# One transformer layer on one core: the low parts of some weights made by ACT and an adding DMA, and two more tiles of FFN 2 as pair jobs

## The chip, the cores and the metric

The kernel runs on one core of one Trainium2 chip. The metric is the device time of one execution in microseconds (us). The time before is 1120.33 us, the median of three runs (1120.18 to 1120.45).

## The reference

One layer of a streaming encoder, batch 1, 512 positions, width 1024, all in float32:

```python
f = swiglu(rms_norm(h, ffn1_pre_g), ffn1_w1, ffn1_w3, ffn1_w2)   # (silu(x@w1) * (x@w3)) @ w2, inner width 2816
h = h + 0.5 * rms_norm(f, ffn1_post_g)
u = rms_norm(h, mix_pre_g)
q, k, v, xr, xg = split(u @ w_in)
y_a = (rg_lru(causal_conv(xr)) * gelu(xg)) @ w_lru_out
y_b = swa_sink_attention(q, k, v, sinks, bias) @ w_attn_out
g = sigmoid(u @ w_gate + b_gate)
merged = g[:, :, 0] * y_a + g[:, :, 1] * y_b
h = h + rms_norm(merged @ w_o, mix_post_g)
f = swiglu(rms_norm(h, ffn2_pre_g), ffn2_w1, ffn2_w3, ffn2_w2)
h = h + 0.5 * rms_norm(f, ffn2_post_g)
```

## The kernel before

**Products in three terms.** Every float32 matrix product is made of three products of reduced float32 (float32r). Each operand x is split into a high part, the rounded copy, and a low part, x minus the high part. The product is wh·xh + wl·xh + wh·xl. A weight tile comes by a raw load of 512 KB on the SP queue (`dma_one`, L142). ACT makes the high part with a copy (L160 in `split_to`, L195 in `split2`), and DVE makes the low part with a subtraction (L161, L196). `get(name, i, ahead)` keeps loads and splits ahead of the use.

**Units.** `unit` makes 128 of the output columns for all 512 positions: 8 slices of the inner dimension times 3 terms, which is 24 matmuls of 128x512 (`mm_feat`, L205 to L207).

**Pairs.** The class `Pairs` treats two tiles of 128 columns together by a Strassen-Winograd scheme. Each weight matrix of such a pair is one job with 7 products in place of 8, each of 12 matmuls of 128x256 (`mm_s`, L845 to L847). `prep(m, i)` makes the weights of job m in five steps: i = 0 the sums S12 and S34 (four DVE operations), 1 the parts of the raw tile itself (`ra`), 2 those of S12, 3 those of S34, 4 those of a quarter (w22). `run` makes a job's products one after the other and calls the steps of the next job in between. The input side (sums of x by `sums`, tiles t1 to t4) is made once.

**Stages.** FFN 1 has 22 tiles: 6 as units, and 16 in 16 pair jobs (`NC1` = 6). The mixing follows (recurrent branch, attention, gates), then w_attn_out ("wao", 8 units from 684.73 us on), w_o ("wo", from 728.25 us), and FFN 2: tiles 0 and 1 at the end of `tok_gemm` for w_o, tiles 2 and 3 as four units (`swiglu_units`, `NC2` = 4), then 18 pair jobs. The gemm with w2 closes each FFN. Some partial products of w2 are made early (`PRE_AT`) and kept in DRAM (pre_w2b).

**Order.** Instructions are issued in the order of the code. `later(n, fn, rank)` puts work off by n points, and `point()` marks them, two in each unit and one after each product of a job. Work tiles come from a pool of 43 slots (`NSLOT`) of 128x1024; a slot is free again when the last reader of its tile is done. GpSimd (POOL) makes few operations: the low part OL of the attention output (L1481), and the issue of some DMAs.

Of the kernel before, what the change touches and what calls it, by code (L numbers as in the profile page):

```python
# [15 lines left out]
P = 128  # L16
# [35 lines left out]
def hybrid_layer(ctx: ExitStack, tc: tile.TileContext, a: dict, out: bass.AP):  # L52
# [22 lines left out]
    def f32(ap):  # L75
        return ap.bitcast(F32)
# [73 lines left out]
    def split_to(n):  # L150
        while st["split"] < min(n, len(order)) and st["split"] not in paired:
            k = st["split"]
            if k in apart:
                st["split"] += 1
                continue
            dma_to(k + 1)
            r = raws.pop(k)
            hi = slot([P, D], F32R, name="whi")
            lo = slot([P, D], F32R, name="wlo")
            act.activation(hi, r, AF.Copy)  # L160
            dve.tensor_tensor(out=lo, in0=r, in1=f32(hi), op=ALU.subtract)  # L161
            pairs[k] = (hi, lo)
            st["split"] += 1

# [14 lines left out]
    def later(n, fn, rank=1):  # L179
        uid[0] += 1  # L180
        due.append((now[0] + n, rank, uid[0], fn))
# [11 lines left out]
    def split2(hi, lo, src):  # L193

        act.activation(hi, src, AF.Copy)  # L195
        dve.tensor_tensor(out=lo, in0=src, in1=f32(hi), op=ALU.subtract)  # L196

    def mm_feat(ps, w, c0=0, c1=SEQ, xh=None, xl=None, ks=range(KT)):

# [11 lines left out]
    def unit(nm, i, **kw):  # L211
        w = get(nm, i)
        ps = bank("f")
        mm_feat(ps, w, **kw)
        return ps
# [269 lines left out]
    def pre_at(where):  # L485
        for nm, f, at_, step in PRE_AT.get(where, ()):
            pre_pair(nm, f, at_, step)
# [298 lines left out]
    def silu_mul(ps1, ps3, R=None, hid=None):  # L786

        t = slot([P, 2, SEQ], name="sw")
        f = len(hid.f) if hid else None
        if f is not None and f in hid.apart:  # L790
            if f - f % 2 not in hid.c:
                hid.c[f - f % 2] = slot([P, 2, SEQ], name="cc")
            o = hid.c[f - f % 2][:, f % 2, :]
        else:
            o = t[:, 1, :]
        if R is None:
            act.activation(t[:, 0, :], ps1, AF.Silu)
            dve.tensor_tensor(out=o, in0=ps3, in1=t[:, 0, :], op=ALU.mult)
        else:
            dve.tensor_tensor(out=t[:, 0, :], in0=ps1, in1=R, op=ALU.mult)  # L800
            dve.tensor_tensor(out=t[:, 1, :], in0=ps3, in1=R, op=ALU.mult)
            act.activation(t[:, 0, :], t[:, 0, :], AF.Silu)
            dve.tensor_tensor(out=o, in0=t[:, 1, :], in1=t[:, 0, :], op=ALU.mult)
        return o
# [45 lines left out]
    class Pairs:  # L850
# [13 lines left out]
        def prep(self, m, i):  # L864
            if m >= len(self.jobs):
                return
            k = self.k0 + 2 * m
            if i == 0:
                if k not in loaded or k + 1 not in loaded:
                    self.raws(m)  # L870
                s12, s34 = slot([P, 2 * QH], name="S12"), slot([P, 2 * QH], name="S34")
                self.w[m] = {"r": (raws.pop(k), raws.pop(k + 1)), "s": (s12, s34)}
            W = self.w[m]
            (ra, rb), (s12, s34) = W["r"], W["s"]
            a11, a12, a21, a22 = ra[:, :QH], ra[:, QH:], rb[:, :QH], rb[:, QH:]

            def both(src, w=2 * QH):
                hi = slot([P, w], F32R, name="whi")
                lo = slot([P, w], F32R, name="wlo")
                split2(hi, lo, src)  # L880
                return hi, lo

            def halves(p, a, b):
                W[a] = p[0][:, :QH], p[1][:, :QH]
                W[b] = p[0][:, QH:], p[1][:, QH:]

            if i == 0:
                dve.tensor_tensor(out=s12[:, :QH], in0=a21, in1=a22, op=ALU.add)
                dve.tensor_tensor(out=s12[:, QH:], in0=s12[:, :QH], in1=a11, op=ALU.subtract)
                dve.tensor_tensor(out=s34[:, QH:], in0=a12, in1=s12[:, QH:], op=ALU.subtract)  # L890
                dve.tensor_tensor(out=s34[:, :QH], in0=a11, in1=a21, op=ALU.subtract)
            elif i == 1:
                halves(both(ra), "a11", "a12")
            elif i == 2:
                halves(both(s12), "s1", "s2")
            elif i == 3:
                halves(both(s34), "s3", "s4")
            elif i == 4:
                t = slot([P, 2, QH], F32R, name="w22")
                split2(t[:, 0, :], t[:, 1, :], a22)  # L900
                W["a22"] = t[:, 0, :], t[:, 1, :]
                del W["r"], W["s"]

        def run(self, tail, hooks={}):
# [4 lines left out]
            for n, (nm, f) in enumerate(self.jobs):  # L909
# [8 lines left out]
                at = lambda i: [f() for f in hooks.get((n, i), ())]  # L918
                mm_s(W["a11"], X["b11"], bu)
                act.activation(q1, bu, AF.Copy)  # L920
                if n == len(self.jobs) - 1:
                    tail()
                at(1)
                mm_s(W["s1"], X["t1"], bx)
                act.activation(q5, bx, AF.Copy)
                at(2)
                last()
                self.prep(n + 1, 1)
                mm_s(W["s2"], X["t2"], bu, True)
                del W["s1"], W["s2"]  # L930
                act.activation(u, bu, AF.Copy)
# [53 lines left out]
    def load_x(k, q=sp):  # L985
        q.dma_start(out=xts[k // 2][:, k % 2, :], in_=a["xT"][k * P : (k + 1) * P, :])

    def load_w(u, kp):
        nm, i = order[u]
        c = slice(kp * 2 * P, (kp + 1) * 2 * P)  # L990
        sp.dma_start(out=raw3[u][:, c], in_=a[nm][i * P : (i + 1) * P, c])


    warm = slot([P, 512], F32R, name="warm")
# [3 lines left out]
        pe.matmul(psw, warm[:, :P], warm, start=True, stop=True)  # L998

    load_x(0, act)  # L1000
    sp.dma_start(out=vec, in_=a["vec"])
    for kp in range(KT // 2):
        load_w(0, kp)
        if kp:
            load_x(2 * kp)
        load_w(1, kp)
        load_w(2, kp)
        load_x(2 * kp + 1)
    dma_to(NS + 2)
# [54 lines left out]
    pairs_a.prep(0, 0)  # L1064
    ps.append(unit("w3a", 1))
    pairs_a.prep(0, 1)
    p1 = unit("w1a", 2)
    pairs_a.prep(0, 2)

# [54 lines left out]
    def swiglu_units(na, nb, f0, f1, hid, R=None, p1=None):  # L1124
        for f in range(f0, f1):
            p1, p3 = p1 or unit(na, f), unit(nb, f)
            later(1, lambda p1=p1, p3=p3: hid.f.append(silu_mul(p1, p3, R, hid)))
            p1 = None

    def uview(hh, th):  # L1130

        return lambda e, k: uT[:, e, 4 * hh + k, th * 256 : th * 256 + 256]
# [1 line left out]
    def pair_view(p):  # L1134
        return lambda e, k: p[e][:, k, :]

    def sums(xf):

        t = [slot([P, 4, 256], name="T") for _ in range(4)]
        dve.tensor_tensor(out=t[0], in0=xf[0, 1], in1=xf[0, 0], op=ALU.subtract)  # L1140
        dve.tensor_tensor(out=t[2], in0=xf[1, 1], in1=xf[0, 1], op=ALU.subtract)
        dve.tensor_tensor(out=t[1], in0=xf[1, 1], in1=t[0], op=ALU.subtract)
        dve.tensor_tensor(out=t[3], in0=xf[1, 0], in1=t[1], op=ALU.subtract)
        return t

    def to_slots(src):
        p = slot([P, 4, 256], F32R, name="Xh"), slot([P, 4, 256], F32R, name="Xl")
        split2(p[0], p[1], src)
        return pair_view(p)
# [363 lines left out]
    w = get("wao", 0)  # L1513
    point(True)
    pre_at("wao")
    xh = [OH[k // 2][:, k % 2, :] for k in range(KT)]
    xl = [OL[k // 2][:, k % 2, :] for k in range(KT)]
    mg = []
# [18 lines left out]
    bs = tok_gemm("wo", mg, KT, RO, "mix_post_g", 1.0, "ffn2_pre_g", [("w1b", 0), ("w3b", 0), ("w1b", 1), ("w3b", 1)], h1, h2, xf=xf)  # L1537


    hid = Hidden("w2b")  # L1540
    X2, tn = {"b11": uview(0, 0), "b21": uview(1, 0), "b22": uview(1, 1)}, []
    later(1, lambda: hid.f.append(silu_mul(bs[0], bs[1])))
    later(2, lambda: hid.f.append(silu_mul(bs[2], bs[3])))
    later(1, lambda: tn.extend(sums(xf)))
    later(2, lambda: xf.clear())
    for i in range(3):
        later(2 + i, lambda i=i: X2.update({f"t{i + 1}": to_slots(tn[i])}))
    pairs_b = Pairs("w1b", "w3b", NC2, X2, hid)
    end = 2 * 2 * (NC2 - 2)
    for i, at_ in enumerate((end - 7, end - 4, end - 3, end - 2, end - 1)):  # L1550
        later(at_, lambda i=i: pairs_b.prep(0, i))
    later(end, lambda: pairs_b.prep(1, 0))
    swiglu_units("w1b", "w3b", 2, NC2, hid)
    point(True)
    X2["t4"] = to_uT(tn[3], 0, 1)
    tn.clear()
    pairs_b.run(w2_ahead)
    X2 = pairs_b = None
    w2_gemm("w2b", hid, "ffn2_post_g", 0.5, None, [], h2, None)


# [9 lines left out]
SCAN_LAG = (1, 2, 3, 4, 6, 7, 9, 10)  # L1571
NSLOT = 43
RO = 6
W2 = {"w2a": (6, (4,), 6, 0.95), "w2b": (2, (4, 4), 4, 0.95)}
TR_K = {"w2a": 2, "wo": 4}
PRE = {"w2b": (2, 4, 6, 8, 14)}
PRE_AT = {"xr": [("w2b", 2, 2, 2), ("w2b", 8, 8, 2)], "xg": [("w2b", 4, 7, 1)], ("wg", 13): [("w2b", 6, 1, 1)], "wao": [("w2b", 14, 4, 1)]}
W2_LOAD = (14, 9, 8, 8)
P0A, P0B = 6, 8
W2_LEAD = 2.5  # L1580
W2_RAW = 4
W2_FLUSH = 2.5

NC1 = 6
NC2 = 4


# [52 lines left out]
```

## Time and profile before

| | us |
|---|---|
| median of three runs | 1120.33 |
| the profiled execution | 1120.09 |
| its span | 1118.3 |
| PE busy | 1109.7 (99%) |
| DVE busy | 907.3 (81%) |
| ACT busy | 607.8 (54%) |
| POOL busy | 34.7 (3%) |

The granted TensorE clock was 0.999 of full speed. A row of a group names the line, the engine, the operation, output<-input, the shapes and the count, then busy time, mean ns of one and the idle time before it. A row of waits gives who waited for what: us in total, times, the longest. A row of the timeline begins with the start and the duration in us. A row of windows begins with the stretch and its length, then has the busy time of PE, PEld (weight loads), DVE, ACT and POOL with their instruction counts, the granted clock, the share of the DMA engines' time and GB/s. A row of DMA issues ends with the KB of one and the median us from issue to landing.

### The profile page before, as it was taken

Reading aid. Unit: us, or ns where it says so; the run is one execution under the profiler, and the core shown is the slowest. Engines: PE = TensorE matmul, PEld = TensorE weight load, DVE = VectorE, ACT = ScalarE, POOL = GpSimd, SP = SyncE. Lnnn points to the kernel's source line nnn. Section 1 sums busy time; section 2 is a strip of 40 time slices with the busy share of each in tenths; the row PEclk is TensorE's granted clock in tenths of the full one; section 3 lists DMA queues with packets and bytes.
Section 4 is the critical chain, followed back from the end, with each engine's and each line's share of the span. In section 5 each row is a group of like instructions: output and inputs, shape, how many; then the busy total and the mean of one; then the engine's idle time right before and its main releaser. Section 6 shows DMA issues by size and latency. Waiting matters only on the chain.

```text
span 1118.3 us, 17215 instructions
## 1 busy us (share of the span) xinstructions
PE 1109.7 (99%) x6613; PEld 987.7 (88%) x6613; DVE 907.3 (81%) x1609; ACT 607.8 (54%) x1072; POOL 34.7 (3%) x60
## 2 busy tenths in 40 slices
PE   9999999999999999999999999999999999999997
PEld 7889999988889887888888888888999999998886
DVE  5999888888887777886799877777868888887995
ACT  7555555564455368945655664355644555555352
POOL 0000000000000000001021111000000000000000
PEclk9999999999999999999999999999999999999999
DMA  9863332260554444536232335562333322357543
GB/s 343 148 165 102 114 96 94 77 225 1 173 203 159 162 156 149 182 117 225 76 95 76 95 95 218 199 241 79 133 121 104 114 90 101 95 205 268 178 177 113
DMA packets 50482, 161.12 MB, mean 144 GB/s; under 512 B 5536, under 2 KB 7072, under 8 KB 50400
## 3 DMA queue, kind: packets, MB, share of 16 engines
q1 hardware_dynamic: 47808, 151.33, 39.3%
q0 software_dynamic: 2448, 8.43, 4.0%
q8 instruction: 52, 0.85, 0.3%
q10 hardware_dynamic: 144, 0.26, 0.1%
q14 instruction: 30, 0.25, 0.1%
HBM read 136.42 MB, written 22.54 MB: 142 GB/s over the span
## 4 chain that ended last, share of the span: by engine, by line
PE 98%; ACT 1%; DMA 1%; DVE 0%; DVEq 0%; issue 0%
PE f L205 12%; PE f L207 12%; PE f L206 12%; PE c L845 10%; PE c L847 10%; PE c L846 10%; PE acc L223 5%; PE acc L224 5%; PE acc L225 5%; PE acc L719 3%; PE acc L721 3%; PE acc L720 3%; PE pt L1446 1%; PE s L1410 1%; DMA t<-pre_w2b 1%; PE tr L294 1%
## 5 line engine op out<-in xcount | busy, mean ns | idle before, releaser
L205 PE MATMUL f<-uT,whi 128*128 128x512 f32 (+1 forms) x536 | 196.7, 367 | 0.0
L207 PE MATMUL f<-uT,whi 128*128 128x512 f32 (+1 forms) x536 | 195.2, 364 | 0.0
L206 PE MATMUL f<-uT,wlo 128*128 128x512 f32 (+1 forms) x536 | 195.1, 364 | 0.0
L205 PEld LDWEIGHTS f<-uT,whi 128*128 128x128 f32 x536 | 101.2, 189 | 16.9 <-issue 1.4
L845 PE MATMUL c<-Xh,whi 128*128 128x256 f32 x408 | 115.6, 283 | 0.1
L847 PE MATMUL c<-uT,whi 128*128 128x256 f32 x408 | 115.5, 283 | 0.0
L846 PE MATMUL c<-Xh,wlo 128*128 128x256 f32 x408 | 115.5, 283 | 0.0
L846 PE MATMUL c<-uT,wlo 128*128 128x256 f32 x408 | 115.5, 283 | 0.0
L847 PE MATMUL c<-Xl,whi 128*128 128x256 f32 x408 | 115.5, 283 | 0.0
L845 PE MATMUL c<-uT,whi 128*128 128x256 f32 x408 | 115.5, 283 | 0.0
L207 PEld LDWEIGHTS f<-uT,whi 128*128 128x128 f32 x536 | 101.1, 189 | 16.2
L206 PEld LDWEIGHTS f<-uT,wlo 128*128 128x128 f32 x536 | 101.2, 189 | 15.6
L196 DVE TENSOR_TENSOR wlo<-S,whi 128x1024 fp32r<-128x1024 f32 x68 | 82.9, 1219 | 16.4 <-ACT whi L195 16.4
L845 PEld LDWEIGHTS c<-Xh,whi 128*128 128x128 f32 x408 | 78.3, 192 | 0.3 <-ACT ct L920 0.3
L846 PEld LDWEIGHTS c<-uT,wlo 128*128 128x128 f32 x408 | 78.3, 192 | 0.0
L845 PEld LDWEIGHTS c<-uT,whi 128*128 128x128 f32 x408 | 78.3, 192 | 0.0
L846 PEld LDWEIGHTS c<-Xh,wlo 128*128 128x128 f32 x408 | 78.3, 192 | 0.0
L847 PEld LDWEIGHTS c<-uT,whi 128*128 128x128 f32 x408 | 78.3, 192 | 0.0
L847 PEld LDWEIGHTS c<-Xl,whi 128*128 128x128 f32 x408 | 78.3, 192 | 0.0
L195 ACT ACTIVATE whi<-S 128x1024 fp32r<-128x1024 f32 x68 | 68.2, 1050 | 0.0
L223 PE MATMUL acc<-whi,hT 128*128 128x512 f32 x160 | 62.5, 390 | 0.0
L224 PE MATMUL acc<-wlo,hT 128*128 128x512 f32 x160 | 62.3, 389 | 0.0
(406 smaller groups left out, 2741.6 us busy)
## 6 DMA issues: line engine op xcount, KB each, us to landing
raw_w2a<-in_w2a_dram SPq DMA_DIRECT2D x22, 512.0 KB, 4.6
raw_w1b<-in_w1b_dram SPq DMA_DIRECT2D x22, 512.0 KB, 4.5
raw_w3b<-in_w3b_dram SPq DMA_DIRECT2D x22, 512.0 KB, 4.5
raw_w3a<-in_w3a_dram SPq DMA_DIRECT2D x21, 512.0 KB, 4.2
raw_w1a<-in_w1a_dram SPq DMA_DIRECT2D x20, 512.0 KB, 4.6
raw_w2b<-in_w2b_dram SPq DMA_DIRECT2D x17, 512.0 KB, 4.1
h<-h SPq DMA_DIRECT2D x16, 512.0 KB, 3.7
raw_wg<-in_wg_dram SPq DMA_DIRECT2D x16, 512.0 KB, 3.9
```

The costliest lines, as they stand in the source:

```text
L195: act.activation(hi, src, AF.Copy)
L196: dve.tensor_tensor(out=lo, in0=src, in1=f32(hi), op=ALU.subtract)
L205: pe.matmul(ps[:, c0:c1], wh[:, s], h_, start=k == 0, stop=False)
L206: pe.matmul(ps[:, c0:c1], wl[:, s], h_, start=False, stop=False)
L207: pe.matmul(ps[:, c0:c1], wh[:, s], l_, start=False, stop=k == KT - 1)
L223: pe.matmul(acc[n], x[:, 0, c], wh[:, s], start=first, stop=False, skip_group_check=True)
L224: pe.matmul(acc[n], x[:, 0, c], wl[:, s], start=False, stop=False, skip_group_check=True)
L225: pe.matmul(acc[n], x[:, 1, c], wh[:, s], start=False, stop=last, skip_group_check=True)
L719: pe.matmul(b, h[:, c], wh, start=start and n_ == 0, stop=False, skip_group_check=True)
L845: pe.matmul(ps, wh[:, s], xh, start=first, stop=False, skip_group_check=True)
L846: pe.matmul(ps, wl[:, s], xh, start=False, stop=False, skip_group_check=True)
L847: pe.matmul(ps, wh[:, s], xl, start=False, stop=k == 3, skip_group_check=True)
```

## The change

- For w_attn_out's units 1 to 6, for FFN 2's first job, and for the raw tile of each job from the fourth on (13 in FFN 1, 17 in FFN 2), the low part is made by `add_low`: ACT writes −x rounded, and a DMA issued by POOL adds x into that tile. DVE subtracted before.
- In `run`, the high part of the next job's raw tile comes right after the first product's copy, and its low part (new step 5) after the second product's copy. Both stood behind the previous job's last product before.
- `NC2` = 2: FFN 2's tiles 2 and 3 become two pair jobs (20 jobs in all). The first job's weights are made at points beside w_attn_out's units (`WAO_PREP`). The sums of x and t1 to t4 are made right after w_o's gemm and in the first job.
- At the start, the first load of the second tile goes to ACT's queue. The partial product of w2 at "wao" begins one point later (`PRE_AT`, 4 becomes 5).

```diff
@@ split_to
             act.activation(hi, r, AF.Copy)
-            dve.tensor_tensor(out=lo, in0=r, in1=f32(hi), op=ALU.subtract)
+            if order[k] in ADD_W:
+                add_low(lo, r)
+            else:
+                dve.tensor_tensor(out=lo, in0=r, in1=f32(hi), op=ALU.subtract)
@@ new
+    def add_low(lo, src):
+
+        act.activation(lo, src, AF.Copy, scale=-1.0)
+        pool.dma_start(out=f32(lo), in_=src, accum_op=ALU.add)
@@ Pairs.prep
             def both(src, w=2 * QH):
                 hi = slot([P, w], F32R, name="whi")
                 lo = slot([P, w], F32R, name="wlo")
-                split2(hi, lo, src)
+                if m == 0 and self.na == "w1b":
+                    act.activation(hi, src, AF.Copy)
+                    add_low(lo, src)
+                else:
+                    split2(hi, lo, src)
                 return hi, lo
...
             elif i == 1:
-                halves(both(ra), "a11", "a12")
+                W["p"] = slot([P, 2 * QH], F32R, name="whi"), slot([P, 2 * QH], F32R, name="wlo")
+                halves(W["p"], "a11", "a12")
+                act.activation(W["p"][0], ra, AF.Copy)
+            elif i == 5:
+                hi, lo = W.pop("p")
+                if m < ADD_FROM and (m or self.na == "w1a"):
+                    dve.tensor_tensor(out=lo, in0=ra, in1=f32(hi), op=ALU.subtract)
+                    return
+                add_low(lo, ra)
@@ Pairs.run
                 act.activation(q1, bu, AF.Copy)
+                self.prep(n + 1, 1)
                 if n == len(self.jobs) - 1:
                     tail()
                 at(1)
                 mm_s(W["s1"], X["t1"], bx)
                 act.activation(q5, bx, AF.Copy)
+                self.prep(n + 1, 5)
                 at(2)
                 last()
-                self.prep(n + 1, 1)
@@ the start
     load_x(0, act)
+    load_w(1, 0, act)
...
-        load_w(1, kp)
+            load_w(1, kp)
@@ before w_attn_out's units
+    pairs_b = Pairs("w1b", "w3b", NC2, X2, hid)
+    for i, at_ in WAO_PREP:
+        later(at_, lambda i=i: pairs_b.prep(0, i), 5)
@@ after w_o
-    swiglu_units("w1b", "w3b", 2, NC2, hid)
-    point(True)
-    X2["t4"] = to_uT(tn[3], 0, 1)
-    tn.clear()
-    pairs_b.run(w2_ahead)
+    tn.extend(sums(xf, X2))
+    xf.clear()
+    hid.f.append(silu_mul(bs[0], bs[1]))
+    X2["t2"] = to_slots(tn[1])
+    pairs_b.prep(1, 0)
+    hid.f.append(silu_mul(bs[2], bs[3]))
+    late = {
+        (0, 2): [lambda: X2.update(t3=to_slots(tn[2]))],
+        (0, 3): [lambda: X2.update(t4=to_uT(tn[3], 0, 1)), tn.clear],
+    }
+    pairs_b.run(w2_ahead, late)
@@ constants
+WAO_PREP = ((-1, 0), (0, 3), (1, 5), (5, 6), (2, 7), (3, 9), (4, 10))
+ADD_W = {("wao", i) for i in range(1, 7)}
+ADD_FROM = 3
-NC2 = 4
+NC2 = 2
```

More of the change, by code (lines that the diff above doesn't have):

```diff
@@ L867, in prep @@
             k = self.k0 + 2 * m
+            if i < 0:
+                dma_one(k)
+                dma_one(k + 1)
+                return
             if i == 0:
@@ L892, in prep @@
             elif i == 1:
-                halves(both(ra), "a11", "a12")
+                W["p"] = slot([P, 2 * QH], F32R, name="whi"), slot([P, 2 * QH], F32R, name="wlo")
[5 more added lines that the diff above has]
+                    dve.tensor_tensor(out=lo, in0=ra, in1=f32(hi), op=ALU.subtract)
+                    return
+                add_low(lo, ra)
             elif i == 2:
@@ L986, in load_x, with load_w @@
         q.dma_start(out=xts[k // 2][:, k % 2, :], in_=a["xT"][k * P : (k + 1) * P, :])
-    def load_w(u, kp):
+    def load_w(u, kp, q=sp):
         nm, i = order[u]
         c = slice(kp * 2 * P, (kp + 1) * 2 * P)
-        sp.dma_start(out=raw3[u][:, c], in_=a[nm][i * P : (i + 1) * P, c])
+        q.dma_start(out=raw3[u][:, c], in_=a[nm][i * P : (i + 1) * P, c])
     warm = slot([P, 512], F32R, name="warm")
@@ L1066, in hybrid_layer @@
     pairs_a.prep(0, 1)
+    pairs_a.prep(0, 5)
     p1 = unit("w1a", 2)
@@ L1135, in pair_view, with sums @@
         return lambda e, k: p[e][:, k, :]
-    def sums(xf):
+    def sums(xf, X=None):
         t = [slot([P, 4, 256], name="T") for _ in range(4)]
@@ L1141, in sums @@
         dve.tensor_tensor(out=t[2], in0=xf[1, 1], in1=xf[0, 1], op=ALU.subtract)
+        if X is not None:
+            X["t1"] = to_slots(t[0])
         dve.tensor_tensor(out=t[1], in0=xf[1, 1], in1=t[0], op=ALU.subtract)
@@ L1515, in hybrid_layer @@
     pre_at("wao")
+    hid = Hidden("w2b")
+    X2, tn = {"b11": uview(0, 0), "b21": uview(1, 0), "b22": uview(1, 1)}, []
+    pairs_b = Pairs("w1b", "w3b", NC2, X2, hid)
+    for i, at_ in WAO_PREP:
+        later(at_, lambda i=i: pairs_b.prep(0, i), 5)
     xh = [OH[k // 2][:, k % 2, :] for k in range(KT)]
@@ L1537, in hybrid_layer @@
     bs = tok_gemm("wo", mg, KT, RO, "mix_post_g", 1.0, "ffn2_pre_g", [("w1b", 0), ("w3b", 0), ("w1b", 1), ("w3b", 1)], h1, h2, xf=xf)
[L1540 to L1552, printed above, removed]
-    swiglu_units("w1b", "w3b", 2, NC2, hid)
-    point(True)
-    X2["t4"] = to_uT(tn[3], 0, 1)
-    tn.clear()
-    pairs_b.run(w2_ahead)
-    X2 = pairs_b = None
+    tn.extend(sums(xf, X2))
[9 more added lines that the diff above has]
+    pairs_b.run(w2_ahead, late)
+    X2 = pairs_b = late = None
     w2_gemm("w2b", hid, "ffn2_post_g", 0.5, None, [], h2, None)
@@ L1576 @@
 PRE = {"w2b": (2, 4, 6, 8, 14)}
-PRE_AT = {"xr": [("w2b", 2, 2, 2), ("w2b", 8, 8, 2)], "xg": [("w2b", 4, 7, 1)], ("wg", 13): [("w2b", 6, 1, 1)], "wao": [("w2b", 14, 4, 1)]}
+PRE_AT = {"xr": [("w2b", 2, 2, 2), ("w2b", 8, 8, 2)], "xg": [("w2b", 4, 7, 1)], ("wg", 13): [("w2b", 6, 1, 1)], "wao": [("w2b", 14, 5, 1)]}
 W2_LOAD = (14, 9, 8, 8)
 P0A, P0B = 6, 8
+ADD_W = {("wao", i) for i in range(1, 7)}
+ADD_FROM = 3
 W2_LEAD = 2.5
```

## The prediction

> **What bounds the kernel now.** I read the page's first part and its chain, then TensorE's (PE's) waits, then windows around the stages that the change touches.
>
> ```profile
> span 1118.3 us, 17215 instructions
> PE 1109.7 (99%) x6613; PEld 987.7 (88%) x6613; DVE 907.3 (81%) x1609; ACT 607.8 (54%) x1072; POOL 34.7 (3%) x60
> PE 98%; ACT 1%; DMA 1%; DVE 0%; DVEq 0%; issue 0%
> ```
>
> PE is busy in 99% of the span and makes 98% of the chain that ended last. What makes the kernel faster is fewer or cheaper matmuls, or a wait of PE that goes. The waits are few:
>
> ```profile
> PEld f L205 <- issue: 1.4, 4, 0.4
> PEld acc L719 <- DMA t<-pre_w2b: 0.5, 1, 0.5
> PEld f L1046 <- ACT uT L1039: 0.4, 1, 0.4
> PEld f L1048 <- DVE uT L1040: 0.3, 1, 0.3
> PEld c L845 <- ACT ct L920: 0.3, 1, 0.3
> ```
>
> Apart from the warm-up these are the longest that lie in stages which the change touches: the start (L1046, L1048), one pair job of FFN 1 (L845), the last gemm (L719). All five rows together are 2.9 us. Next, the stages by window (columns: PE, PEld, DVE, ACT, POOL busy with instruction counts, clock, DMA share, GB/s):
>
> ```profile
> 684.73:728.30 43.57, 43.57 (x194) 36.09 (x193) 32.58 (x43) 17.72 (x25) 2.56 (x3) 1.00 0.61 221
> 720.00:742.00 22.00, 22.00 (x99) 18.23 (x98) 17.93 (x20) 11.75 (x14) 1.08 (x2) 1.00 0.98 365
> 798.69:820.47 21.78, 21.78 (x98) 18.02 (x97) 15.20 (x19) 7.32 (x9) 0.00 (x0) 1.00 0.28 102
> 820.47:1002.00 181.53, 181.53 (x1514) 181.52 (x1513) 148.25 (x218) 94.58 (x156) 0.00 (x0) 1.00 0.33 106
> ```
>
> The first is w_attn_out's eight units, the second the turn to w_o, the third FFN 2's four units of tiles 2 and 3, the fourth its 18 pair jobs. PE fills each of them to the last hundredth. DVE (VectorE) is at 82% in the pair jobs, but nothing waits for it there, so DVE time saved is worth nothing by itself.
>
> **Matmuls: four units become two pair jobs.** A unit is 24 matmuls of 128x512; the four took 21.78 us (the third window), 0.2269 us a matmul. A pair job is 84 matmuls of 128x256. One job, from first matmul to first matmul:
>
> ```profile
> 889.59 0.28 PE L845 MATMUL c<-uT,whi 128*128 128x256 f32 x1
> ...
> 899.67 0.28 PE L845 MATMUL c<-uT,whi 128*128 128x256 f32 x1
> 899.79 0.28 PE L846 MATMUL c<-uT,wlo 128*128 128x256 f32 x1
> ```
>
> That is 10.08 us, or 0.120 us a matmul, and two jobs are 20.16 us. The term is 20.16 − 21.78 = **−1.62 us**. It lies wholly on PE, so it counts in full if the new job's operands are there in time. The Trainium skill ("TensorE: Matmul & The Clock Gate", section "Wait — 56ns, not 53.3ns?") gives a warm start-to-start of N ÷ 2.4 GHz and about 2.5 ns, so by that rule, as an estimate, the two jobs would save 2.37 us, not 1.62. The trace disagrees with 226.9 and 120.0 ns at a granted clock of 1.00, so the measured pitch decides.
>
> **Low parts by ACT and an adding transfer.** The change takes 39 subtractions of 128x1024 off DVE (13 in FFN 1's jobs, 6 for w_attn_out, 3 in FFN 2's first job, 17 in its other jobs), and adds 39 ACT copies and 39 transfers issued by POOL (GpSimd), each of which adds 512 KB into a tile.
>
> ```profile
> L195 ACT ACTIVATE whi<-S 128x1024 fp32r<-128x1024 f32 x68 | 68.2, 1050 | 0.0
> L196 DVE TENSOR_TENSOR wlo<-S,whi 128x1024 fp32r<-128x1024 f32 x68 | 82.9, 1219 | 16.4 <-ACT whi L195 16.4
> L890 DVE TENSOR_TENSOR S<-raw_w1b,S 128x512 f32<-128x512 f32 x8 | 5.5, 693 | 0.3
> ```
>
> DVE loses 39 × 1.219 = 47.5 us, ACT gains 39 × 1.050 = 41.0 us; both have room (148.25 and 94.58 of 181.53 us in the jobs, some 17 × 1.2 us less and 17 × 1.05 us more now). On PE's path this is 0, with one condition: the sum must land before PE reads the tile. ACT's place in a steady job, first before, then after (ct are the copies of the products that leave PSUM, L920, L925 and L931 before; whi and wlo the parts of raw_w3b, the next job's first weight):
>
> ```order
> 695 L920 ACTIVATE ct_8712<-c_8714 128x256
> 696 L925 ACTIVATE ct_8712<-c_8715 128x256
> 697 L195 ACTIVATE whi_8756<-raw_w3b_1856_8585 128x1024
> 698 L931 ACTIVATE ct_8712<-c_8714 128x256
> 699 L195 ACTIVATE whi_8773<-S_1870_8702 128x1024
> ```
>
> ```order
> 733 L944 ACTIVATE ct_8853<-c_8855 128x256
> 734 L911 ACTIVATE whi_8871<-raw_w3b_1861_8725 128x1024
> 735 L950 ACTIVATE ct_8853<-c_8856 128x256
> 736 L203 ACTIVATE wlo_8872<-raw_w3b_1861_8725 128x1024
> 737 L956 ACTIVATE ct_8853<-c_8855 128x256
> ```
>
> The high part moved ahead of the second ct, and the negative copy stands behind it. With the times of the job that starts at 889.59:
>
> ```profile
> 891.29 0.38 ACT L920 ACTIVATE ct<-c 128x256 f32<-128x256 f32 x1
> 892.67 0.38 ACT L925 ACTIVATE ct<-c 128x256 f32<-128x256 f32 x1 [1.00 <-PE c L847]
> 894.39 1.05 ACT L195 ACTIVATE whi<-raw_w1b 128x1024 fp32r<-128x1024 f32 x1
> 895.47 1.23 DVE L196 TENSOR_TENSOR wlo<-raw_w1b,whi 128x1024 fp32r<-128x1024 f32 x1 [0.87 <-ACT whi L195]
> 889.66 0.80 SPq L142 DMA_DIRECT2D raw_w1b<-in_w1b_dram  x2
> ```
>
> After: first ct ends at 891.67, high part at 892.72, second ct at 893.1, negative copy at 894.15, so POOL can issue at about 894.2. The next job's second matmul (L846) reads the low part at 899.79, and its weight load begins a little sooner. So the transfer has about **5.6 us** from issue to landing. Before, DVE was done at 896.7, with 3.1 us to spare. No adding transfer is in this trace. The nearest rows, medians from issue to landing:
>
> ```profile
> BT<-bias_scr POOLq DMA_DIRECT2D x16, 128.0 KB, 3.6
> bc_ffn_post_g<-in_ffn_post_g_dram POOLq DMA_DIRECT2D x2, 512.0 KB, 6.1
> bc_mix_post_g<-in_mix_post_g_dram POOLq DMA_DIRECT2D x1, 512.0 KB, 8.0
> raw_w1b<-in_w1b_dram SPq DMA_DIRECT2D x22, 512.0 KB, 4.5
> ```
>
> The 8.0 ran in the window 720 to 742, whose DMA share is 0.98. The 6.1 is POOL's own 512 KB, but it spreads one 4 KB row over all partitions. The 4.5 is a plain 512 KB load of SP's; an adding transfer must read its target as well, but its source is on the chip. I take 4.8 us, nearest to SP's row, because the two raw loads that a job issues (889.66, 4.5 us to landing) are over when the sum starts: no stall. The ends are 3.6 and 8.0 us, which is 0 or 2.4 us in each of the jobs that follow. The Trainium skill ("SBUF — State Buffer", section "Who interferes with whom") warns that a DVE instruction with two SBUF inputs contends with GpSimd's reads and that descriptor writing can starve behind DVE; no run here shows it, and it would push toward the upper end.
>
> A raw tile's slot now comes free when the sum lands, not when DVE is done. The SP queue's later loads stand behind that slot, but they serve a job further on: 0, at most a few tenths.
>
> **w_attn_out.** The sums of units 1 and 2 now stand ahead of the last OL on POOL. Before, then after (OL is the attention output's low part, which PE reads in unit 0):
>
> ```order
> 45 L1481 TENSOR_TENSOR OL_6738<-o_6916,OH_6737 128x2x128
> 46 L1481 TENSOR_TENSOR OL_6738<-o_6986,OH_6737 128x2x128
> 47 L248 DMA bc_mix_post_g_7419<-in_mix_post_g_dram 128x1024
> 48 L248 DMA bc_ffn_pre_g_7421<-in_ffn_pre_g_dram 128x1024
> ```
>
> ```order
> 58 L1510 TENSOR_TENSOR OL_6751<-o_6929,OH_6750 128x2x128
> 59 L204 DMA wlo_6957<-raw_wao_1486_6765 128x1024
> 60 L204 DMA wlo_7010<-raw_wao_1511_6847 128x1024
> 61 L1510 TENSOR_TENSOR OL_6751<-o_7000,OH_6750 128x2x128
> 62 L204 DMA wlo_7060<-raw_wao_1530_6908 128x1024
> ```
>
> ```profile
> 685.08 1.04 ACT L160 ACTIVATE whi<-raw_wao 128x1024 fp32r<-128x1024 f32 x1
> 686.03 0.40 ACT L1480 ACTIVATE OH<-o 128x256 fp32r<-128x256 f32 x1
> 686.51 1.48 POOL L1481 TENSOR_TENSOR OL<-o,OH 128x256 fp32r<-128x256 f32 x1 [7.41 <-ACT OH L1480]
> 725.86 0.56 POOL L248 DMA_DIRECT2D bc_mix_post_g<-in_mix_post_g_dram  x1 [37.87 <-PE f L207]
> ```
>
> Before, OL ended at 687.99. Unit 0 starts at 684.73 and needs it for its 21st matmul, 684.73 + 20 × 0.227 = 689.27: 1.3 us to spare. After, ACT's copy for unit 2 comes ahead of OH (+1.05), and POOL issues that sum (0.56 us) ahead of OL, which then ends at 689.2 to 689.6. I put **+0.2** (0 to +0.5). The sums of units 1 to 5 are two units (10.9 us) ahead of their use; unit 6's has the least room.
>
> **FFN 2's first job beside w_attn_out.** Its DVE sums (4 × 0.69), ACT copies and three sums go to points of that stage, where DVE is at 32.58 of 43.57 us. Six low parts less on DVE there (−7.3) pay for the sums. DMA is what gets tight: share 0.61 before, and nine sums more. At the 365 GB/s that 0.98 of the engines moved, 512 KB is 1.4 us of all engines; read twice, 2.8, and nine are 13 to 25 us against 17 idle. Then w_o's loads (the window at 0.98) come later. The price lies between 0 and some 4 us; I take 0, since w_o's weights are loaded ahead and its first units find theirs split.
>
> **The rest.** X's sums and t1 to t4 move from beside the four units to just ahead of and inside the first job. In the third window DVE had 6.6 us idle and ACT 14.5, so the cover is there; if it were not, the late ones would be t1 to t3, at some tenths each. The first load of the second tile on ACT's queue brings SP's later loads of the start forward by one issue: 0 to −0.7 (L1046, L1048), taken as −0.2, and up to +0.4 if ACT is late by its issue. The later start of one partial w2 pass moves it off the same engines: 0.
>
> **The sum**: −1.62 + 0.2 − 0.2 = −1.6 us. The profiled execution took 1120.09 us, 0.24 below the median and 1.8 over its span; it becomes 1118.5, and by the median 1120.33 − 1.6 = **1118.7 us**. A measurement of this kernel can tell about 0.2%, 2.24 us, from no change, so the forecast lies within it.
>
> **Rivals.** *Sums land late in the pair jobs* (0.20): 13 jobs of FFN 1 and 17 of FFN 2 would each wait for the low part of their first weight. It decides from 5.6 us. At 6.1 each waits 0.5 us: 30 × 0.5 − 1.6 = +13, 1134 us; at 8.0, 30 × 2.4 − 1.6 = +70, 1191 us. For it speaks POOL's 6.1 row; against it SP's 4.5 and the free engines (DMA share 0.33). *The middle is late* (0.18): OL, unit 6's sum or w_o's loads take 1 to 5 us from the gain: 1119.5 to 1123.5; for it speaks the share of 0.98 at 720 to 742, against it that PE waits for no load there now. *More waits go* (0.12): the start's 0.7 and L845's 0.3 with it: −1.62 − 1.0 = −2.6, 1117.7 us. That needs the rows L1046, L1048 and L845 to vanish together. *The two jobs don't save what they should* (0.04): if the new first job waits as long for its operands as it saves, 1120.3. My forecast has 0.46.
>
> **How the numbers follow.** Faster by over 0.2%: the third rival and a little: 0.13. Slower by over 0.2%: nearly all of the first, and a third of the second with stalls over 3.8 us, and mixtures: 0.29. Within: 0.58. The range starts at 1117.8 (the third rival's upper part) and ends at 1132, where the first rival's sums land at 6.0 us; about 0.07 and 0.12 lie outside. The likeliest case's own range is 1118.0 to 1119.5.
>
> **What would show it.** Right: two more jobs of 10.08 us each from about 798, no PE wait named after POOL's transfers, sums of 4 to 5.5 us to landing, DVE some 47 us less busy. Wrong: PEld waits at L846 for a wlo by DMA, jobs longer than 10.08 us, waits in the w_o units, or sums of 6 us and more.

## The result and the profile after

The changed kernel took 1134.5 us (median of four, 1132.69 to 1136.57) where the kernel before took 1120.37: a ratio of 1.0127 (95% interval 1.0112 to 1.0142), slower by 14 us. The forecast was 1118.7 us, its range ended at 1132. The profiled execution took 1135.16 us. From the page of the changed kernel, the first part and the chain:

```profile
span 1133.4 us, 17545 instructions
PE 1113.8 (98%) x6685; PEld 992.5 (88%) x6685; DVE 873.8 (77%) x1589; ACT 649.8 (57%) x1122; POOL 67.6 (6%) x99
PE 84%; issue 6%; DMA 6%; DVE 2%; ACT 2%; SPq 0%; DVEq 0%; POOLq 0%; ACTq 0%; POOL 0%
```

DVE is 33.5 us less busy (47.5 less for the low parts, more for the two new jobs) and ACT 42 us more. But PE makes only 84% of the chain now: waits stand between its matmuls. The waits of PE's weight loads in the changed kernel:

```profile
PEld f L214 <- DMA wlo<-raw_wao: 5.4, 2, 4.2
PEld c L854 <- DMA wlo<-raw_w1a: 3.8, 3, 2.0
PEld c L854 <- DMA wlo<-raw_w3a: 3.3, 3, 1.3
PEld c L854 <- DMA wlo<-raw_w3b: 0.8, 1, 0.8
```

All four are for a low part that an adding transfer makes: in w_attn_out (wao), in FFN 1 (w1a, w3a) and a little in FFN 2 (w3b). The next two fences give the stages by window, of before and of after: FFN 1's jobs, w_attn_out's units, the stretch up to FFN 2's first job, FFN 2's jobs. In before the third stretch includes the four units.

```profile
72.43:234.02 161.59, 161.53 (x1345) 161.32 (x1344) 137.20 (x223) 94.75 (x153) 0.00 (x0) 1.00 0.34 110
684.73:728.25 43.52, 43.52 (x193) 36.05 (x192) 32.55 (x42) 17.67 (x25) 2.56 (x3) 1.00 0.61 221
728.25:820.47 92.22, 92.22 (x513) 80.47 (x512) 68.30 (x123) 48.54 (x88) 0.00 (x0) 1.00 0.42 153
820.47:1001.90 181.43, 181.43 (x1513) 181.42 (x1512) 148.15 (x218) 94.48 (x156) 0.00 (x0) 1.00 0.33 106
```

```profile
72.42:243.04 170.62, 164.75 (x1346) 163.22 (x1345) 122.42 (x210) 107.03 (x166) 11.20 (x13) 0.99 0.54 144
693.72:744.10 50.38, 45.78 (x193) 37.03 (x192) 29.12 (x41) 26.98 (x35) 7.64 (x9) 0.97 0.99 277
744.10:814.27 70.17, 70.17 (x418) 62.37 (x416) 55.28 (x109) 39.73 (x78) 1.10 (x2) 1.00 0.46 174
814.27:1016.97 202.70, 202.11 (x1682) 201.70 (x1681) 146.22 (x227) 122.74 (x192) 14.62 (x17) 1.00 0.54 148
```

FFN 1 is 9.0 us longer, w_attn_out 6.9. The third stretch is 70.17 against 92.22 − 21.78 = 70.44. FFN 2 has 20 jobs in 202.70, which is 1.1 more than 181.43 + 20.16. So 9.0 + 6.9 + 1.1 − 0.3 − 1.6 = 15.1 us, the difference of the two profiled executions. The 1.6 us of the matmuls came; 17 us were lost elsewhere. The DMA share is the other thing to see: it rose from 0.61 to 0.99 in w_attn_out.

**FFN 1.** The adding transfers, called sums from here on, as they landed (KB, median us from issue to landing):

```profile
wlo<-raw_w1b POOLq DMA_DIRECT2D x9, 512.0 KB, 4.4
wlo<-raw_w3b POOLq DMA_DIRECT2D x9, 512.0 KB, 4.4
wlo<-raw_w3a POOLq DMA_DIRECT2D x7, 512.0 KB, 5.1
wlo<-raw_w1a POOLq DMA_DIRECT2D x6, 512.0 KB, 5.5
wlo<-raw_wao POOLq DMA_DIRECT2D x6, 512.0 KB, 6.3
```

4.4 us in FFN 2, more in FFN 1. One late sum in FFN 1, in rows of three engines: SP issues a raw load, POOL the sum 0.2 us later, PE gets the low part 7.5 us after that.

```profile
168.02 0.33 SPq L142 DMA_DIRECT2D raw_w1a<-in_w1a_dram  x1
168.21 0.86 POOL L204 DMA_DIRECT2D wlo<-raw_w1a  x1 [9.23 <-PE c L855]
175.70 0.39 PE L854 MATMUL c<-Xh,wlo 128*128 128x256 f32 x1 [1.84 <-DMA wlo<-raw_w1a]
176.04 0.40 PE L853 MATMUL c<-Xh,whi 128*128 128x256 f32 x1
176.25 0.41 PE L854 MATMUL c<-Xh,wlo 128*128 128x256 f32 x1
```

Look at the last two rows too: after the wait the matmuls start 0.21 us apart, not 0.12. The row of windows for the stretch behind it has a granted clock of 0.50:

```profile
176.04:179.45 3.41, 3.41 (x19) 3.41 (x18) 2.31 (x4) 1.26 (x2) 0.00 (x0) 0.50 0.42 154
```

So this wait costs a second time: 16 matmuls at the slow pitch are some 1.5 us. The clock fell nowhere else in FFN 1's jobs. In their window PE was idle for 170.62 − 164.75 = 5.9 us. The remaining 1.6 of the 9.0 us are also delays at the late sums: the profile counts a matmul as busy for 0.28 us though the next one starts after 0.12, and the matmul behind a wait takes 0.1 us more.

PE waited for six of FFN 1's 13 sums. Four of them, in the tenth to the thirteenth job, stood beside SP's raw loads and took 6.3 to 7.5 us. The two others, issued at 106.40 and 136.89, took 5.6 and 6.4 us, and no raw load ran beside them between their first 1.6 us and their last 0.4. In the time of each, the answer on DMA has one packet of instructions, that is of the program itself, on a queue of its own (packets, MB, share of the 16 engines; here from 136.89 to 143.33):

```profile
q8 instruction: 1, 0.02, 1.0%
```

The sum at 857.86 in FFN 2, 6.2 us to landing, has such a packet too, but so has the one at 939.30, which took 4.4. So this second cause is a lead that no run tested.

**w_attn_out.** Between 699 and 706 us SP and POOL issue nine transfers of 512 KB. The answer on DMA for that window, with the median to landing:

```profile
raw_w1b<-in_w1b_dram SPq DMA_DIRECT2D x2, 512.0 KB, 8.9
wlo<-raw_wao POOLq DMA_DIRECT2D x2, 512.0 KB, 10.2
raw_wao<-in_wao_dram SPq DMA_DIRECT2D x2, 512.0 KB, 13.1
rawp<-in_w2b_dram SPq DMA_DIRECT2D x2, 512.0 KB, 13.9
raw_wo<-in_wo_dram SPq DMA_DIRECT2D x1, 512.0 KB, 13.3
```

What followed, one row each of DVE, ACT, POOL and PE:

```profile
710.55 0.69 DVE L904 TENSOR_TENSOR S<-raw_w1b 128x512 f32<-128x512 f32 x1 [8.30 <-DMA raw_w1b<-in_w1b_dram]
714.71 0.63 ACT L1559 ACTIVATE mg<-g 128x512 fp32r<-128x512 f32 x1 [11.29 <-DVE g L1557]
719.43 0.85 POOL L204 DMA_DIRECT2D wlo<-raw_wao  x1 [1.04 <-ACT wlo L203]
725.08 0.50 PE L214 MATMUL f<-OH,wlo 128*128 128x512 f32 x1 [3.74 <-DMA wlo<-raw_wao]
```

DVE stands 8.3 us at the first of its own operations for the first job (S12 and S34, step 0). Behind it in DVE's order is the gated product g, for which ACT stands 11.3 us; behind that in ACT's order are the copies of w_attn_out's next tile, and its sum is issued at 719.43, 1.5 us before PE wants it.

### The profile page after: what moved, and what is told of

Its sections match the earlier page's. It is cut to its first block, busy times and chain, and to the rows that moved or that the text cites. A ratio compares the mean times of both kernels' runs of the same rounds, so it can differ in the third digit from the quotient of the medians.

```text
span 1133.4 us, 17545 instructions
## 1 busy us (share of the span) xinstructions
PE 1113.8 (98%) x6685; PEld 992.5 (88%) x6685; DVE 873.8 (77%) x1589; ACT 649.8 (57%) x1122; POOL 67.6 (6%) x99
## 3 DMA queue, kind: packets, MB, share of 16 engines
q0 software_dynamic: 8064, 28.88, 13.2%
## 4 chain that ended last, share of the span: by engine, by line
PE 84%; issue 6%; DMA 6%; DVE 2%; ACT 2%; SPq 0%; DVEq 0%; POOLq 0%; ACTq 0%; POOL 0%
PE f L213 10%; PE f L214 10%; PE f L215 10%; PE c L854 8%; PE c L853 8%; PE c L855 8%; PE acc L232 4%; PE acc L231 4%; PE acc L233 4%; PE acc L728 3%; PE acc L727 3%; PE acc L729 3%; DMA wlo<-raw_w3a 2%; DMA raw_w3a<-in_w3a_dram 2%; PE pt L1475 1%
## 5 line engine op out<-in xcount | busy, mean ns | idle before, releaser
L213 PE MATMUL f<-uT,whi 128*128 128x512 f32 (+1 forms) x504 | 184.2, 366 | 0.0
L215 PE MATMUL f<-uT,whi 128*128 128x512 f32 (+1 forms) x504 | 182.6, 362 | 0.0
L214 PE MATMUL f<-uT,wlo 128*128 128x512 f32 (+1 forms) x504 | 182.6, 362 | 0.0
L854 PE MATMUL c<-Xh,wlo 128*128 128x256 f32 x432 | 123.6, 286 | 5.8 <-DMA wlo<-raw_w1a 3.2
L854 PE MATMUL c<-uT,wlo 128*128 128x256 f32 x432 | 122.5, 283 | 0.6 <-DMA wlo<-raw_w3b 0.5
L853 PE MATMUL c<-Xh,whi 128*128 128x256 f32 x432 | 123.0, 285 | 0.0
L855 PE MATMUL c<-Xl,whi 128*128 128x256 f32 x432 | 122.9, 285 | 0.0
L855 PE MATMUL c<-uT,whi 128*128 128x256 f32 x432 | 122.4, 283 | 0.0
L853 PE MATMUL c<-uT,whi 128*128 128x256 f32 x432 | 122.3, 283 | 0.0
L213 PEld LDWEIGHTS f<-uT,whi 128*128 128x128 f32 x504 | 95.1, 189 | 15.8 <-issue 1.4
L215 PEld LDWEIGHTS f<-uT,whi 128*128 128x128 f32 x504 | 95.1, 189 | 14.9
L214 PEld LDWEIGHTS f<-uT,wlo 128*128 128x128 f32 x504 | 95.2, 189 | 14.3
L855 PEld LDWEIGHTS c<-uT,whi 128*128 128x128 f32 x432 | 82.9, 192 | 0.1
L853 PEld LDWEIGHTS c<-uT,whi 128*128 128x128 f32 x432 | 82.9, 192 | 0.0
```

What stands on the lines that cost most here:

```text
L213: pe.matmul(ps[:, c0:c1], wh[:, s], h_, start=k == 0, stop=False)
L214: pe.matmul(ps[:, c0:c1], wl[:, s], h_, start=False, stop=False)
L215: pe.matmul(ps[:, c0:c1], wh[:, s], l_, start=False, stop=k == KT - 1)
L853: pe.matmul(ps, wh[:, s], xh, start=first, stop=False, skip_group_check=True)
L854: pe.matmul(ps, wl[:, s], xh, start=False, stop=False, skip_group_check=True)
L855: pe.matmul(ps, wh[:, s], xl, start=False, stop=k == 3, skip_group_check=True)
```

## The experiments

Each was measured beside the kernel before, which lay between 1120.4 and 1120.7 us.

**ffn1_sub: FFN 1 by subtraction.**

```diff
-                if m < ADD_FROM and (m or self.na == "w1a"):
+                if self.na == "w1a" or (m < ADD_FROM and m):
```

> As the changed kernel, but the low parts of FFN 1's 13 raw tiles come from DVE's subtraction again (at the new place); everything else stays. Theory: in FFN 1 the sums take 5 to 7.5 us to land, because SP's raw loads run beside them, and PE waits 9.0 us for them there; those 9.0 us go, so about 1134.5 - 9.0 = 1125.5 us, with jobs of 10.08 us in FFN 1 and the middle and FFN 2 as they were. Rival (the sums burden the DMA engines everywhere, and places only shift): less than 5 us go, 1129.5 us or more.

1126.43 us, 8.1 less. FFN 1 is back at its time of before, w_attn_out is not (windows of this kernel):

```profile
72.53:234.28 161.75, 161.69 (x1346) 161.38 (x1345) 136.61 (x223) 94.56 (x153) 0.00 (x0) 1.00 0.33 110
685.00:736.14 51.14, 45.75 (x193) 37.02 (x192) 29.88 (x43) 28.33 (x37) 7.66 (x9) 0.97 0.99 284
```

The 9.0 us of FFN 1 are the sums', and each stage loses by itself.

**mid_sub: no sums in the middle.**

```diff
-ADD_W = {("wao", i) for i in range(1, 7)}
+ADD_W = set()
...
-                if m == 0 and self.na == "w1b":
+                if False:
...
-                if m < ADD_FROM and (m or self.na == "w1a"):
+                if m < ADD_FROM:
```

> As the changed kernel, but w_attn_out's units 1 to 6 and FFN 2's first job have their low parts from DVE; the sums in the later pair jobs stay, and so do the first job's place and loads. Theory (the nine sums clog the DMA engines between 699 and 719 us, and the loads behind them hold DVE, ACT and POOL): the 6.9 us lost in w_attn_out's units go, about 1127.6 us. Rival (the first job's raw loads, put early into that stage, are enough to hold DVE and with it the units' low parts, whoever makes these): at least 4 us of it stay, 1131.5 us or more.

1132.04 us, only 2.5 less. The waits for sums in w_attn_out went, but there are waits for DVE in their place (below, in no_sums), and in this run FFN 1 lost 0.9 more. The rival has the size right, and its reason in part: without these sums DVE still stands 3.1 us for the first job's raw load. Take the whole middle, from w_attn_out's first unit to FFN 2's first job. The changed kernel spent 50.38 + 70.17 = 120.6 us there, 6.6 more than before without the four units (43.52 + 70.44 = 114.0). mid_sub spent 117.5, so 3.5 us of the 6.6 stay without the nine sums.

**no_sums: not one sum, two more pair jobs.** As mid_sub, and `if True:` for the subtraction in every job.

> As the changed kernel without any adding transfer: all 39 low parts by DVE's subtraction, two more pair jobs and the first job's weights beside w_attn_out as changed. Theory: only the 1.6 to 1.9 us of the matmuls remain, 1118.5 to 1118.8 us. Rival (the first job's place costs by itself): 1121 to 1125 us, lost in w_attn_out's units. Rival (DVE lacks the time in FFN 2's first jobs without sums): jobs 0 to 2 longer than 10.08 us.

1123.43 us: the rival. All 20 jobs of FFN 2 take 10.08 us without a sum, so DVE has the time there. The middle has not (the waits of PE from 685 to 805 us):

```profile
PEld tr L302 <- DVE hg L292: 1.5, 1, 1.5
PEld acc L231 <- DVE g L1556: 1.5, 1, 1.5
PEld acc L232 <- DVE wlo L164: 1.1, 1, 1.1
PEld f L214 <- DVE wlo L164: 1.1, 1, 1.1
```

So the first job's place costs by itself. The middle took 118.9 us here, 5.0 more than before. DVE stands 3.5 us for the first job's raw load and then has that job's 7.2 us of work, and it is late by 1 to 1.5 us at four places. Between them, mid_sub and no_sums leave 1.6 to 3.1 of the 6.6 us to the nine sums themselves.

**sums_only: the kernel before with the sums of the pair jobs alone.** `prep` and `run` as changed, `NC2` = 4.

> The kernel before with the adding transfers in the pair jobs alone (13 in FFN 1, 15 in FFN 2, weights in the changed order); FFN 2's tiles 2 and 3 stay units, w_attn_out stays as it was. Theory: FFN 1 loses 9.0 us and FFN 2 about 1.0, so 1120.4 + 10 = 1130.4 us. Rival (FFN 1 was late because of the changed start, not of the sums): 1121 to 1123 us.

1131.13 us: FFN 1 took 170.16 us, w_attn_out its old 43.52, FFN 2's 18 jobs 183.24, 1.8 more than before. The start is not to blame.

```profile
73.12:243.28 170.16, 164.74 (x1346) 163.21 (x1345) 122.60 (x210) 107.01 (x166) 11.21 (x13) 0.99 0.54 144
```

**loads_behind: FFN 1's loads behind the sum.** All 39 sums, but the loads of a job go to the queue of the sum, after it.

```diff
                 self.prep(n + 1, 5)
+                if self.na == "w1a":
+                    st["q"] = pool
+                    self.raws(n + 2)
+                    st["q"] = sp
...
-                self.raws(n + 3)
+                if self.na != "w1a" or n >= len(self.jobs) - 3:
+                    self.raws(n + 3)
```

> As the changed kernel, with all its 39 sums, but FFN 1's raw weight loads of the later jobs go to POOL's queue, right behind the sum of their job, where SP issued them beside it. Theory (SP's raw loads that run beside the sum stretch it from 4.4 to 6.5 to 7.5 us): behind the sum they can't, the sums land in about 4.5 us, and most of the 9.0 us of FFN 1 go: 1126 to 1128 us, unless the loads, now later, make a job wait themselves. Rival (the sum is slow in FFN 1 for another reason, DVE's two-input operations above all): the sums stay at 5 to 7.5 us and the time at 1133 us or more.

FFN 1 took 163.54 us in place of 170.62:

```profile
72.41:235.95 163.54, 162.78 (x1346) 161.88 (x1345) 123.60 (x210) 107.06 (x166) 25.38 (x39) 1.00 0.56 151
686.63:740.26 53.63, 47.41 (x194) 38.18 (x192) 32.11 (x44) 29.32 (x37) 7.68 (x9) 0.94 0.99 288
```

```profile
wlo<-raw_w3a POOLq DMA_DIRECT2D x7, 512.0 KB, 5.4
wlo<-raw_w1a POOLq DMA_DIRECT2D x6, 512.0 KB, 5.4
```

The same sums and the same bytes, in another order and queue, and 7.1 of the 9.0 us are gone. So the cause of most of the loss in FFN 1 is where the raw loads stand against the sums. They still run in the sums' time, though:

```profile
167.89 0.89 POOL L204 DMA_DIRECT2D wlo<-raw_w1a  x1 [8.19 <-PE c L855]
168.45 1.41 POOL L142 DMA_DIRECT2D raw_w3a<-in_w3a_dram  x2
```

The loads follow 0.6 and 1.1 us behind the sum, and nearly every sum beside such loads takes 5.4 us, not the expected 4.5, which lies at the edge. Whether the later issue or the other queue helps was not separated. DVE is as busy as in the changed kernel (123.60 and 122.42 us), which speaks against the rival. The time is 1130.96 us and not 1127, since w_attn_out lost 10.1 us here (53.63 us): PE waits 3.6 and 2.7 us for the sums of two units. Why they are longer than in the changed kernel, which does the same there, was not followed up.

**first_sums, unit_sums, late_prep: which sums cost in the middle.** None has sums in the pair jobs from the second on. first_sums keeps the three of the first job, unit_sums the six of w_attn_out's units, late_prep all nine with the first job's steps four points later:

```diff
-WAO_PREP = ((-1, 0), (0, 3), (1, 5), (5, 6), (2, 7), (3, 9), (4, 10))
+WAO_PREP = ((-1, 0), (0, 7), (1, 9), (5, 10), (2, 11), (3, 13), (4, 14))
```

> As the changed kernel, but sums only for the three low parts of FFN 2's first job; w_attn_out's units and all other jobs by DVE. Theory (without sums DVE is late by about 1 us at four places of w_attn_out and w_o; the three sums of the first job have some 70 us until their use, so DVE gains 3.7 us there and no PE wait can come of the sums): 2 to 4 us less than without any sum (1123.4), so 1119.5 to 1121.5 us. Rival (any sum in that stage clogs the loads): 1124 us or more.

> As the changed kernel, but sums only for w_attn_out's units 1 to 6; the first job's weights by DVE at the same points. Theory (the unit's sum stood behind the first job's sum in POOL's order, and both behind the first job's raw load on ACT and DVE): POOL's part of that goes, but ACT and DVE still stand behind the raw load, so w_attn_out's units lose 2 to 6 us: 1121 to 1125 us. Rival (POOL's order alone): they lose under 1 us, 1119 to 1120 us.

> As the changed kernel without sums in the pair jobs (which makes 1126.4 less about 1 us), with the nine sums of the middle, but the steps of the first job four points (two units) later, while its raw loads are issued at the same point. Theory (DVE, ACT and POOL stand behind the first job's raw load): with the load landed by then nothing waits, and w_attn_out's units lose under 1.5 us: 1119 to 1121 us. Rival (the nine sums and the loads fill the DMA engines, wherever the steps stand): 1123 us or more.

first_sums 1122.25, unit_sums 1123.8, late_prep 1131.26 us. unit_sums is within its theory, and PE waits 3.1 us for one unit's sum there. first_sums lies between theory and rival: 1.2 us less than no_sums, not 2 to 4, and the intervals of the two overlap. For late_prep the theory fell. The windows of w_attn_out in unit_sums and in late_prep, then a DVE row of late_prep:

```profile
684.77:732.89 48.12, 45.45 (x193) 37.09 (x192) 30.14 (x41) 23.92 (x31) 5.11 (x6) 0.96 0.82 237
685.00:735.21 50.21, 45.29 (x194) 37.01 (x192) 26.18 (x37) 24.60 (x32) 6.79 (x8) 0.97 0.88 251
```

```profile
712.44 0.69 DVE L431 TENSOR_TENSOR T<-rawp,rawp 128x512 f32<-128x512 f32 x1 [8.04 <-DMA rawp<-in_w2b_dram]
```

w_attn_out takes 44.34 us with the first job's three sums, 48.12 with the units' six and 50.21 with all nine, where no_sums takes 44.89. So the units' sums are what costs there. In late_prep DVE stands 8.0 us for rawp, another load of the same burst. w_attn_out is as slow as in the changed kernel (50.38), so its loss does not hang on the place of the first job's steps: with a DMA share of 0.88 the loads of the burst land late, and DVE waits for whichever it meets first. With the steps later, another 6.2 us were lost behind w_attn_out (76.33 against 70.17). My theory for this run was wrong, the rival right.

**no_sums_late, two_sums_late, no_sums_gap, no_sums_split: can the gain be kept?** All without sums in the pair jobs from the second on. no_sums_late moves S12, S34 and the quarter (steps 2, 3, 4) of the first job to the turn to w_o. two_sums_late moves S34 and the quarter there and makes the low parts of the raw tile and of S12 by sums. no_sums_gap moves the three steps into DVE's gap behind the splits of w_o. no_sums_split moves S34 and the quarter behind t2, and also takes back the new order of weights inside the jobs and the new start.

> As no_sums (every low part by DVE), but the first job's S12, S34 and quarter are split only at the turn to w_o, ahead of w_o's last four tiles, so that DVE has 3.1 us less among w_attn_out's last units. Theory (without sums only DVE's backlog after 713 us costs): the waits of about 1 us at w_attn_out's last unit and at w_o's first tiles go, 1119 to 1121 us. Rival (DVE's 7 us of the first job don't fit ahead of w_o's transposes wherever they stand): 1122.5 us or more, with the wait moved to w_o's tiles or to the transposes.

> As no_sums, but the first job's raw tile and S12 by sums beside w_attn_out's units, and S34 and the quarter split by DVE at the turn to w_o. DVE has 4.3 us less among w_attn_out's last units and 1.9 us more at the turn. Theory: 1118.8 to 1120.5 us, if two sums of which nothing urgent waits cost nothing. Rival: as for no_sums_late.

> As no_sums_late, but the three steps stand behind the splits of w_o's and of FFN 2's first four tiles, where DVE has a gap of 3.3 us before the first norm in the profile of before (744.9 to 748.2). Theory: nothing waits for them there, 1118.5 to 1120 us, the 1.6 us of the matmuls kept. Rival (ACT's three copies, 2.7 us, delay the first norm, which sets the transposes): 1121 us or more, with PE waiting for the transposes.

> As no_sums, but only the raw tile and S12 of the first job are split beside w_attn_out's units; S34 and the quarter are split after w_o's transposes, right behind t2, and t3 is made ahead of the second job's sums. The order of weights inside the jobs and the loads at the start are those of the kernel before. Theory (DVE's work for the first job, 7.2 us, has to be spread so that no in-order backlog reaches a PE operand): the waits of about 1 us in w_attn_out and w_o go, 1118.7 to 1120.3 us. Rival (DVE is as tight after the transposes): 1121.5 us or more, with the waits at the first job's third to fifth product.

1122.27, 1123.07, 1123.55 and 1121.22 us: none reached its theory. two_sums_late and no_sums_gap came out as the rival, the other two between. The wait moved each time. In no_sums_late, then in no_sums_gap:

```profile
PEld acc L232 <- DVE wlo L164: 3.3, 4, 1.5
```

```profile
PEld tr L302 <- DVE hg L292: 3.4, 1, 3.4
```

In all these runs the first job's raw loads were issued at the same point beside w_attn_out. An earlier or later point for them was not tried.

**pre_earlier and pre_later_only: the partial product of w2.** The first takes no_sums_split's start back from point 5 to 4, the second moves it to 5 in the kernel before.

> As no_sums_split, but the partial product of w2 at w_attn_out begins at point 4, as in the kernel before, not at 5. Theory (the later point, priced at nothing in the prediction, pushes its four DVE splits into the turn to w_o, where PE then waits 1.2 us for the gated product g and some tenths for w_o's low parts): those 2 us go, about 1119.2 us, faster than before by 0.1%. Rival (the first job's DVE work costs the same wherever the partial product stands): 1121 us or more, with the waits moved to earlier units.

> The kernel before with only this partial product begun at point 5 in place of 4. Theory: with no first job beside it the turn to w_o has room, 1120.4 to 1121 us. Rival (the later point alone costs the wait of 1.2 us): 1121.5 us or more.

1120.1 us (ratio to before 0.9997, 0.9988 to 1.0006), between theory and rival, and 1120.39 us (0.9999, 0.999 to 1.0008), the theory. The later point alone costs nothing, as the prediction had it; with the first job beside it, it seems to cost 1.1 us (1121.22 to 1120.1), but these are two separate comparisons whose intervals overlap. pre_earlier is the best version tried, and it cannot be told from the kernel before. Its profiled execution, at 1121.55 us the slowest of its eleven, has 1.7 us of waits for hg and 1.5 for g in w_o; what would take these away was not tried.

## Why the prediction was wrong

Two terms that the prediction took at nothing failed: the wait for the adding transfers in the pair jobs, which measured 9.0 + 1.1 = 10.1 us, and the price of the middle, which measured 6.6.

**The matmuls: right.** −1.6 us was forecast; with −0.3 in the third stretch it came out so, at 10.08 us a job. By the rule of the Trainium skill ("TensorE: Matmul & The Clock Gate", section "Wait — 56ns, not 53.3ns?") they would have saved 2.37 us, as an estimate; no run shows that.

**The transfer's price: the step that failed.** The prediction took 4.8 us, "nearest to SP's row, because the two raw loads that a job issues (889.66, 4.5 us to landing) are over when the sum starts: no stall". Alone the sum took 4.4, so the value was good, and in FFN 2 only two of 17 were late. But the reason was read from one job of FFN 2 and carried over to FFN 1, whose loads start at another place in the job. The kernel before shows it in FFN 1's tenth job, by its first matmul and its second raw load:

```profile
162.02 0.28 PE L845 MATMUL c<-Xh,whi 128*128 128x256 f32 x1
166.53 0.33 SPq L142 DMA_DIRECT2D raw_w1a<-in_w1a_dram  x1
```

The load is issued 4.5 us into the job. By the prediction's own times (889.59 and 894.2) the sum would be issued 4.6 us into it. In the tenth to the thirteenth job of the changed kernel SP's loads do stand beside the sum, which then takes 6.3 to 7.5 us. The point of decision, 5.6 us, was close: a sum that landed 5.6 us after its issue held PE up by 0.26 us.

**The middle: the size was in the working and was not taken.** The prediction put nine sums at 13 to 25 us of all DMA engines against 17 idle, and took 0. The page of each kernel gives the price: POOL's queue (q0) took 4.0% of 1118.3 us before and 13.2% of 1133.4 us after, 105 us more for 39 sums, **2.7 us each**. The windows of FFN 1 agree: the DMA share went from 0.34 of 161.59 to 0.54 of 170.62 us, 37 us for 13 sums, 2.9 us each. So nine are 24 to 26 us, the upper end, and beyond what was idle. "w_o's weights are loaded ahead" looked at the wrong consumer: DVE stood first, at the first job's step 0, and ACT and POOL behind it. w_attn_out lost 6.9 us.

**First job beside w_attn_out.** "Six low parts less on DVE there (−7.3) pay for the sums" held only while adding transfers made these low parts. Without them the first job's place costs 3.5 to 5 us (mid_sub and no_sums), so what the middle lost has two causes.

**OL and the start.** OL's place on POOL made no wait in the profile (0.2 forecast), and the start's 0.2 us did not come: the first pair job begins at 72.42 us, as before (72.43).

**The rivals.** The first, sums late in the pair jobs, at a chance of 0.20, is what happened, though after six of FFN 1's 13 sums and two of FFN 2's 17, not in 30 jobs. The second, the middle late, at 0.18, happened as well. They were weighed as alternatives, but both hang in part on one thing, what else the DMA engines move; their sum, 10.1 + 6.6, lies past the range. What neither rival had was the second price of a long wait, the lower clock: some 1.5 of FFN 1's 9.0 us and 1.6 of the 6.9 in w_attn_out.

## What to carry to other kernels

Where a transfer replaces an engine's operation, read the DMA engines in every stage where it will stand, job by job, and not in one that looks typical. The loads that made FFN 1's sums late stood in the trace of before. The margin is set by what else is issued in those few microseconds. Price it in time of all the DMA engines as well as in us to landing, and when its own numbers fill what is idle, forecast the wait. DVE was 81% busy and no wait of PE was for it in the pair jobs, so the relief was worth nothing there, and the cure had a cost.

## What the runs showed of the hardware

A 512 KB adding transfer within the chip took 4.4 us from issue to landing alone, 6.3 to 7.5 us beside SP's raw loads in FFN 1, and up to 10.2 us in the burst beside w_attn_out. POOL spent 0.86 us on its issue (0.56 on a plain one), and by the estimates above it took 2.7 to 2.9 us of all 16 DMA engines. The plain 512 KB loads of raw_w1b have 4.5 us to landing in the kernel before.

PE's wait of 1.84 us at 175.70 was followed by matmuls 0.20 to 0.21 us apart for 3.4 us; the waits up to 1.31 us in FFN 1 were not. After the wait of 3.74 us in w_attn_out the 128x512 matmuls ran like this:

```profile
725.69 0.63 PE L213 MATMUL f<-OH,whi 128*128 128x512 f32 x1
726.12 0.63 PE L214 MATMUL f<-OH,wlo 128*128 128x512 f32 x1
726.54 0.63 PE L215 MATMUL f<-OL,whi 128*128 128x512 f32 x1
```

They start 0.43 us apart in place of 0.227. The Trainium skill ("TensorE: Matmul & The Clock Gate", section "Why this matters for your kernels") asks for no idle gaps of PE over some 3 us; here the clock fell already behind a wait of 1.84 us. Its 426.7 ns for 512 columns at the low clock (section "Wait — 56ns, not 53.3ns?") agrees with the 0.43 us of these rows.
